# Branch b of a hybrid block in one kernel: its weights prepared by whole rows and stored by GpSimd, its products ordered by output pair, and w_out's banks taken in another order

## The chip, the cores and the metric

The kernel runs on one core of a Trainium2 chip. The metric is the device time of one execution in microseconds (us), lower is better. A core has five engines that run their own instruction streams: TensorE (PE, matrix products, with PEld for its weight loads), VectorE (DVE, elementwise work), ScalarE (ACT, activations and copies), GpSimd (POOL) and SyncE (SP, here only an issuer of DMAs). ScalarE and GpSimd issue DMAs too; a DMA is issued in the order of its engine's stream. TensorE writes into PSUM, of which there are eight banks of 128 x 512 float32; operands lie in SBUF, in tiles of 128 partitions.

## The reference

One layer of a hybrid block on x of 1024 x 1024 float32: a mixer and a SwiGLU network, each with a norm before and behind it. What the change touches is the mixer:

```python
def mixer(h, w_in, b_f, conv_w, w_branch, w_out):
    proj = jnp.einsum("bsd,dn->bsn", h, w_in)
    q, k, v, f_logit, g_b, g_c, hc, gate_conv, gate_attn = jnp.split(proj, _SPLITS, axis=-1)
    ya = g_b * causal_depthwise_conv(g_c * hc, conv_w)
    ...
    yb = forgetting_attention(q.reshape(shp), k.reshape(shp), v.reshape(shp), logf)
    yb = yb.reshape(bsz, s_len, ATTN_WIDTH)
    ya_d = jnp.einsum("bsc,cd->bsd", ya, w_branch[0])
    yb_d = jnp.einsum("bsc,cd->bsd", yb, w_branch[1])
    merged = jax.nn.sigmoid(gate_conv) * ya_d + jax.nn.sigmoid(gate_attn) * yb_d
    return jnp.einsum("bsd,de->bse", merged, w_out)
```

`yb` is 1024 x 512, `w_branch[1]` 512 x 1024, `w_out` 1024 x 1024.

## The kernel before, in words

**Arithmetic.** Each float32 product is made of three matmuls on rounded halves: an operand is split into a high half (a rounding copy by ScalarE) and a low half (a subtraction by VectorE), `split` (L132), and `mm3` (L137) multiplies high by high, high by low and low by high. The large products go by Strassen and Winograd: the operands are cut into 2 x 2 blocks, and seven products of sums of blocks (A11 B11, A12 B21, S1 T1, S2 T2, S3 T3, S4 B22, A22 T4) take the place of eight. A matmul has 128 x 128 weights and 128 x 512 data. All instructions of these helpers are put down to line 77 in the profile, so its rows are told apart by their tiles.

**Stages.** First the norm and v; then 18 jobs of the input projection (L1031: four of q and k, six of the convolution, eight of the gates, the last one run into the attention); attention with branch a's products as filler (L1341); branch b (L1502 to L1570); the w_out stage (L1722); then the feed-forward network.

**Order.** The instructions of an engine run in a fixed order. A planner lays it down at build time from its own costs, except where `strict` names the engine or a call is `pinned` (L119): those instructions keep the order of the program. In the jobs only a few are pinned; in the attention all engines are; in branch b from L1527 on only TensorE is. So VectorE's, ScalarE's and SyncE's orders in the jobs and in branch b are the planner's. An instruction that waits holds up all that stands behind it on its engine.

**Side work in the jobs.** While a job's 84 matmuls run, weights for later stages are prepared. `wo_load` (L965) loads four blocks of w_out, cuts sums and halves, and stores them to `wo_dram`; `wb_load` (L992) does the same for `w_branch[1]`: eight times four DMAs of a 128 x 128 block into a tile `br` (tag "p", two buffers), four sums of 128 x 128 on VectorE, a split of 128 x 896 into `bh` and `bl` (tag "cb", two buffers), and two stores to `wb_dram` issued by ScalarE, 512 bytes a piece. They are run in jobs 2 to 9. `cb_of` (L746) loads a row of forget sums, broadcast to 128 partitions, into buffers of the same tag "cb"; for the first head pair this is called at job 12 (L1068), ahead of the weight loads of that job, which `pairs.get()` (L679) issues one job ahead of use.

**Branch b.** The weights of the seven products (o = A11 to S4) come back from `wb_dram` by `load_wbr` (L1277): the high half into a ring of four buffers (`hi_t`), the low half into a ring of three (`lo_t`), for S1 into a tile of its own. `prod_b` (L1488) makes the product of o for one pair u of output blocks: 6 matmuls. The products run one after the other, each over u = 0 to 3: A11, S1, S2, S3, S4, A22, A12. Two sets of four PSUM banks, `pbanks` and `vbanks`, hold partial sums; `p_s`, `u_s`, `v_s` are copies of them in SBUF. After S3, S4, A22 and A12 VectorE adds the bank and merges: times the gate `sg` (loaded by SyncE into four buffers, `gate`, L1481), added to `um`. Each output block of `um` is done by one of these four products: S3 and S4 finish the columns n1, A22 and A12 the columns n2.

**The w_out stage** begins with `first(0)` (L1621): its bank comes from a new pool of four (`pk`, L1579) that lies on the first four of the eight banks of branch b's pool, and must wait until the last reader of that bank is done. Before, the eight banks were given in the order: three to branch a, four `pbanks`, four `vbanks`, the last three of them on banks 0, 1 and 2.

Of the kernel before, what the change touches and what calls it, by code (L numbers as in the profile page):

```python
# [10 lines left out]
F32 = mybir.dt.float32  # L11
# [6 lines left out]
P = 128  # L18
S = 1024
# [21 lines left out]


B11, B21, B22, T1, T2, T3, T4 = range(7)
A11, A12, A22, S1, S2, S3, S4 = range(7)


@with_exitstack
def block_kernel(
# [83 lines left out]
    def split(hi, lo, src):  # L132

        copy(hi, src)
        sub(lo, src, f32(hi))
# [23 lines left out]
    pre_dram = [dpool.tile([2, P, NC], F32, name=f"pre_dram{f}") for f in range(NPRE)]  # L159
    ri_dram = [dpool.tile([2, S], F32, name=f"ri_dram{j}") for j in range(4)]  # L160
    wo_dram = dpool.tile([7, 4, P, 2, NC], F32, name="wo_dram")
    wb_dram = dpool.tile([7, 2, P, 4, 2, P], F32, name="wb_dram")
    sg_dram = [dpool.tile([2, P, S], F32, name=f"sg_dram{d}") for d in range(8)]

    cw = cpool.tile([P, 4, 4], F32, name="cw")[:, :3, :]
# [372 lines left out]
    def kblk(t):  # L538
        return t.rearrange("p (a b) -> p a b", b=P)
# [7 lines left out]
    def hi_t():  # L547
        return wtile("hi", 4, F32R)
# [416 lines left out]
    def wo_load(n):  # L965
# [23 lines left out]

        return cut, store  # L990

    def wb_load(n):  # L992

        u, kk = divmod(n, 2)
        r = kblk(t0_.tile([P, S], F32, tag="p", name="br", bufs=2))
        h, l = (kblk(t0_.tile([P, S], F32R, tag="cb", name=x, bufs=2)) for x in ("bh", "bl"))
        blocks_ = ((kk, 2 * u + 1), (kk, 2 * u), (2 + kk, 2 * u), (2 + kk, 2 * u + 1))
        for slot, (row, col) in enumerate(blocks_):
            pinned(
                lambda: nc.sync.dma_start(  # L1000
                    r[:, slot],
                    w_branch[0, 1][row * P : (row + 1) * P, col * P : (col + 1) * P],
                ),
                "sync",
            )

        def cut():
            add(r[:, 4], r[:, 0], r[:, 3])
            sub(r[:, 6], r[:, 1], r[:, 0])
            sub(r[:, 5], r[:, 4], r[:, 1])  # L1010
            sub(r[:, 7], r[:, 2], r[:, 5])
            split(h[:, 1:], l[:, 1:], r[:, 1:])

        def store():
            for hl, t in enumerate((h, l)):
                nc.scalar.dma_start(
                    wb_dram[:, hl, :, u, kk, :].rearrange("o p m -> p o m"), f32(t[:, 1:])
                )

        return cut, store  # L1020
# [3 lines left out]
    def do(f, *args):  # L1024
        return lambda: f(*args)

    zts = {}
    h1b = [hB11, hB21, hB22]
    for hh, hl in (hT12, hT34):
        h1b += [(hh[:, b], hl[:, b]) for b in range(2)]  # L1030
    for ij, (kind, j, _, _) in enumerate(jobs):  # L1031
# [12 lines left out]
        if ij < 2:  # L1044
            if ij == 0:
                r1 = raw_t()
                nc.sync.dma_start(r1, kmaj(wcols(jobs[1][2])))
                t0_.tile([P, S], F32, tag="p", name="room", bufs=2)
                h1, l1 = (
                    kblk(t0_.tile([P, S], F32R, tag="cb", name=n, bufs=2)) for n in ("h1", "l1")  # L1050
                )
                split(h1, l1, r1)
                heads = [prep_first(None, t) for t in ((r0, h0, l0), (r1, h1, l1))]
                for _ in range(2):
                    bank(psm, "spare")
                strict[0] = ("tensor", "scalar")
                firsts = strassen_firsts([w for w, _ in heads], h1b, psm, pp)
                strict[0] = ()
            (w, r1), (c11, p1) = heads[ij], firsts[ij]
            w = {**w, **prep_rest(wcols(jobs[ij][3]), r1)}  # L1060
            if ij == 1:
                pairs.q.append(pairs.prep(*pairs.srcs.popleft()))
            _, c12, c21, c22 = strassen(w, h1b, psm, pp, p1, mid)
        elif ij < len(jobs) - 1:
            if ij == 12:
                k_load(0)
                q_load(0)
                cb_of(0, 0)  # L1068
                cb_of(0, 1)
            c11, c12, c21, c22 = strassen(pairs.get(), h1b, psm, pp, None, mid)  # L1070
        else:
            w = pairs.get()
            psm_close()
            strict[0] = engines
            pss, pss_close = pool("pss", space=PSUM)
            c11, c12, c21, c22 = last_pair(w)
# [41 lines left out]
            pinned(store, "scalar")  # L1118
        if ij < len(jobs) - 2:
            side[ij + 1].append(wo_load(ij))  # L1120
        if 1 <= ij < 9:
            side[ij + 1].append(wb_load(ij - 1))
    pp_close()
    w0_close()
    h_close()
# [149 lines left out]
        return t.rearrange("p (k a) b -> p k (a b)", k=2)  # L1275

    def load_wbr(o):  # L1277
        h = hi_t()
        l = kblk(z_tile("wbl", F32R)) if o == S1 else lo_t()
        wb[o] = h, l  # L1280
        for hl, t in enumerate((h, l)):
            nc.sync.dma_start(
                f32(t).rearrange("p (u k) m -> p u k m", u=4), wb_dram[o, hl]
            )

    low_k, up_k = slice(0, 2), slice(2, 4)
    yb11, yb12 = yb[:, low_k, n2], yb[:, low_k, n1]
# [41 lines left out]
        at[t].append(do(load_sg, d))  # L1329
    at[18] += [do(cb_of, 3, 0, True), do(cb_of, 3, 1, True)]  # L1330
    at[20].append(form_t1)
    for o, t in ((A11, 19), (S1, 20), (S2, 24), (S3, 25)):
        at[t].append(do(load_wbr, o))
    rows = {9: 0, 15: 1, 21: 2}
    for t, j in rows.items():
# [152 lines left out]
    def prod_b(ps, o, u, b, first):  # L1488
        (wh, wl), (bh, bl) = wb[o], tb[b]
        kw = {} if first else dict(skip_group_check=True)  # L1490
        for k in range(2):
            m = 2 * u + k
            mm3(
                ps, (wh[:, m, :], wl[:, m, :]), (bh[:, k, :], bl[:, k, :]),
                first and k == 0, k == 1, **kw,
            )

    def merge(d, ns, t, c, sg):
        mul(t, c, sg)
        add(um[:, d, ns], um[:, d, ns], t)  # L1500

    for m in branch_a(KT - 1, 0, psm, "mm"):  # L1502
        pass
    for n in range(2):
# [13 lines left out]
    for u in range(4):  # L1518
# [4 lines left out]
            sub(yb22, yb22, yb11)  # L1523
        if u == 1:
            split(*tb[T2], yb22)
    load_wbr(S4)
    strict[0] = ("tensor",)  # L1527
    divide(3, 1)
    yh1, yl1 = halves_of(1)
# [13 lines left out]
        load_wo(B11, u)  # L1543
    load_wbr(A22)
    for u in range(4):
        prod_b(pbanks[u], S2, u, T2, False)
        copy(u_s[u], pbanks[u])
    load_wbr(A12)
    for u in range(4):
        sg = gate(2 * u + 1, n1)  # L1550
        prod_b(pbanks[u], S3, u, T3, False)
        add(v_s[u], v_s[u], pbanks[u])
        merge(2 * u + 1, n1, v_s[u], v_s[u], sg)
    for u in range(4):
# [606 lines left out]
```

## Time and profile before

| | us |
|---|---|
| median of 3 runs | 1340.06 (1337.64 to 1340.38) |
| profiled execution | 1339.44 |
| its span, first to last instruction | 1337.7 |
| TensorE busy | 1308.7 (98%) |
| VectorE busy | 983.8 (74%) |
| ScalarE busy | 567.8 (42%) |
| GpSimd busy | 141.8 (11%) |

In a row of a timeline stand the start from the span's start, the duration, the engine, the operation, out<-in, and in brackets the idle time of the engine before it with what ended it; a q behind the engine's name (SPq, ACTq) is its queue of DMA issues. In a table by windows each engine has its busy time and count, then come the clock granted to TensorE (1.00 is full), the mean share of the DMA engines, and GB/s. A matmul's own duration (0.39 us) is longer than the step to the next one, since they are pipelined.

### The profile page before, as it was taken

The numbers are of one execution on the slowest core, as the hardware profiler recorded it, in microseconds if no ns is written. First come the engines' busy times: TensorE is split into PE (matmuls) and PEld (weight loads), VectorE is DVE, ScalarE is ACT, GpSimd is POOL, SyncE is SP. The second block draws the span as 40 slices with busy tenths as digits, with TensorE's granted clock in tenths as the row PEclk, the third lists the DMA queues.
The fourth block names the chain that finished last, engine by engine and source line by source line (L and its number), as shares of the span: only waits on it lengthen the run. The fifth ranks groups of instructions, "written<-read, shape, count | busy, mean of one in ns | idle before, by whom it ended". The sixth has DMA issues, their size and how long they took to land.

```text
span 1337.7 us, 18116 instructions
## 1 busy us (share of the span) xinstructions
PE 1308.7 (98%) x6686; PEld 1087.5 (81%) x6686; DVE 983.8 (74%) x1549; ACT 567.8 (42%) x902; POOL 141.8 (11%) x271
## 2 busy tenths in 40 slices
PE   9999999979999999997999999999999999999998
PEld 8988877768888888886888888888888888888886
DVE  6975889756555877578599689897677766677585
ACT  6642333324335766443577523232222323444452
POOL 0011000001102212001012112220011101000000
PEclk9999999989999999998999999999999999999999
DMA  6337667686555544598256645553233327876541
GB/s 219 114 116 195 195 184 208 168 226 170 163 152 183 192 135 138 180 340 321 93 190 220 189 150 173 182 180 96 101 116 105 108 98 264 315 272 194 158 165 63
DMA packets 223817, 235.14 MB, mean 176 GB/s; under 512 B 12512, under 2 KB 169248, under 8 KB 223728
## 3 DMA queue, kind: packets, MB, share of 16 engines
q1 hardware_dynamic: 163456, 157.13, 37.7%
q0 software_dynamic: 16496, 54.83, 11.2%
q10 hardware_dynamic: 43776, 22.02, 6.3%
q8 instruction: 52, 0.85, 0.3%
q14 instruction: 37, 0.30, 0.1%
HBM read 161.79 MB, written 72.16 MB: 175 GB/s over the span
## 4 chain that ended last, share of the span: by engine, by line
PE 77%; issue 13%; DMA 4%; DVE 4%; ACT 1%; POOL 1%; SPq 0%; DVEq 0%; POOLq 0%; ACTq 0%
PE b L77 42%; PE pd L77 16%; PE pba L77 3%; PE pv L77 3%; PE p L77 2%; PE po L77 2%; PE tps L77 2%; PE sp L77 2%; PE pbp L77 1%; DMA wb_dram<-bl 1%; PE ma L77 1%; PE q L77 1%; PE tp L77 1%; DMA lo<-qk_dram 1%; DMA raw<-in_w_in_dram 1%
## 5 line engine op out<-in xcount | busy, mean ns | idle before, releaser
L77 PE MATMUL b<-x,hi 128*128 128x512 f32 x1088 | 335.5, 389 | 0.0
L77 PEld LDWEIGHTS b<-x,hi 128*128 128x128 f32 x1088 | 204.1, 188 | 42.4
L77 PE MATMUL b<-x,lo 128*128 128x512 f32 x544 | 211.7, 389 | 0.0
L77 DVE TENSOR_TENSOR c<-c,b 128x512 f32<-128x512 f32 x193 | 131.0, 680 | 50.3 <-PE b L77 43.6
L77 DVE TENSOR_TENSOR lo<-raw,hi 128x1024 fp32r<-128x1024 f32 x90 | 108.2, 1202 | 71.5 <-PE b L77 61.2
L77 ACT ACTIVATE hi<-raw 128x1024 fp32r<-128x1024 f32 (+1 forms) x96 | 97.2, 1015 | 85.1 <-PE b L77 46.4
L77 PEld LDWEIGHTS b<-x,lo 128*128 128x128 f32 x544 | 102.1, 188 | 21.1
L77 ACT ACTIVATE hi<-sx 128x1024 fp32r<-128x1024 f32 (+1 forms) x42 | 43.7, 1040 | 137.0 <-PE b L77 122.7
L77 ACT ACTIVATE sgf<-c 128x512 f32<-128x512 f32 x31 | 19.6, 632 | 131.6 <-DVE c L77 112.5
L77 DVE TENSOR_TENSOR sx<-raw 128x512 f32<-128x512 f32 x78 | 53.5, 686 | 29.3 <-DMA raw<-in_w_in_dram 19.9
L77 DVE TENSOR_TENSOR lo<-sx,hi 128x1024 fp32r<-128x1024 f32 (+1 forms) x42 | 50.3, 1197 | 25.7 <-PE b L77 24.0
L77 PE MATMUL pd<-hi,lo 128*128 128x512 f32 x160 | 62.3, 389 | 0.0
L77 PE MATMUL pd<-hi 128*128 128x512 f32 x160 | 61.9, 390 | 0.0
L77 PE MATMUL b<-hT12h,lo 128*128 128x512 f32 x136 | 54.0, 397 | 6.5 <-DVE lo L77 6.5
L77 PE MATMUL pd<-ghi 128*128 128x512 f32 x148 | 57.6, 389 | 0.0
L77 PE MATMUL pd<-ghi,glo 128*128 128x512 f32 x148 | 57.6, 389 | 0.0
L77 PE MATMUL pd<-glo,ghi 128*128 128x512 f32 x148 | 57.6, 389 | 0.0
L77 PE MATMUL b<-hT34h,hi 128*128 128x512 f32 x136 | 53.4, 393 | 1.6 <-DVE c L77 1.6
L77 PE MATMUL b<-hT12h,hi 128*128 128x512 f32 x136 | 53.6, 394 | 0.0
L77 PE MATMUL b<-hT12l,hi 128*128 128x512 f32 x136 | 53.6, 394 | 0.0
L77 PE MATMUL b<-hT34l,hi 128*128 128x512 f32 x136 | 53.0, 389 | 0.0
L77 PE MATMUL b<-hT34h,lo 128*128 128x512 f32 x136 | 52.9, 389 | 0.0
(456 smaller groups left out, 3047.9 us busy)
## 6 DMA issues: line engine op xcount, KB each, us to landing
raw<-in_w_gate_up_dram SPq DMA_DIRECT2D x55, 512.0 KB, 3.9
raw<-in_w_in_dram SPq DMA_DIRECT2D x35, 512.0 KB, 5.4
x<-wo_dram SPq DMA_DIRECT2D x28, 512.0 KB, 7.2
a_dramS<-um POOLq DMA_DIRECT2D x44, 256.0 KB, 3.0
a_dramA<-um POOLq DMA_DIRECT2D x33, 256.0 KB, 2.8
sg<-sg_dram SPq DMA_DIRECT2D x32, 256.0 KB, 3.8
wo_dram<-h ACTq DMA_DIRECT2D x16, 448.0 KB, 4.6
wo_dram<-l ACTq DMA_DIRECT2D x16, 448.0 KB, 7.0
```

The source lines that it names most:

```text
L77: ins = getattr(self.engine, name)(*args, **kw)
```

## The change

Four things. (1) `wb_load` loads two whole rows of blocks (128 x 1024 each) at n = 0 and n = 4 and works on them in four steps each: split A12 and A22; split A11 and make the four sums in place; split S2 and S3; split S4 and S1. The names' numbers are changed so that the pairs lie side by side in `wb_dram`, now in pieces of 2 KB, and the stores are issued by GpSimd. The work lies in jobs 2 to 5 and 10 to 13. (2) The first `cb_of` loads move from job 12 to job 15, behind `pairs.get()`. (3) In branch b, S2, S4 and S3 run pair by pair, then A22 and A12 pair by pair; S4's weights are loaded during the attention in place of S3's, S3's behind A11's products, and A12's go into two buffers of the tag "raw" (three buffers, which B11's and T1's data held before). (4) Five unused banks are taken first, so that `pbanks` are banks 0 to 3 and `vbanks` banks 4 to 7.

```diff
-A11, A12, A22, S1, S2, S3, S4 = range(7)
+A11, A12, A22, S2, S3, S4, S1 = range(7)
...
-    wb_dram = dpool.tile([7, 2, P, 4, 2, P], F32, name="wb_dram")
+    wb_dram = dpool.tile([7, 2, P, 2, NC], F32, name="wb_dram")
...
     def wb_load(n):
-        u, kk = divmod(n, 2)
-        r = kblk(t0_.tile([P, S], F32, tag="p", name="br", bufs=2))
-        h, l = (kblk(t0_.tile([P, S], F32R, tag="cb", name=x, bufs=2)) for x in ("bh", "bl"))
-        blocks_ = ((kk, 2 * u + 1), (kk, 2 * u), (2 + kk, 2 * u), (2 + kk, 2 * u + 1))
-        for slot, (row, col) in enumerate(blocks_):
-            pinned(
-                lambda: nc.sync.dma_start(
-                    r[:, slot],
-                    w_branch[0, 1][row * P : (row + 1) * P, col * P : (col + 1) * P],
-                ),
-                "sync",
-            )
+        kk, c = divmod(n, 4)
+        if c == 0:
+            wrows[:] = [t0_.tile([P, S], F32, tag="p", name="br", bufs=2) for _ in range(2)]
+            for row, t in zip((kk, 2 + kk), wrows):
+                pinned(
+                    lambda: nc.sync.dma_start(t, w_branch[0, 1][row * P : (row + 1) * P, :]),
+                    "sync",
+                )
+        (r11, r21), (r12, r22) = (
+            [t.rearrange("p (u x m) -> x p u m", x=2, m=P)[x] for x in range(2)] for t in wrows
+        )
+        h, l = (t0_.tile([P, S], F32R, tag="cb", name=x, bufs=2) for x in ("bh", "bl"))
+        width = NC if c == 1 else S
+        first = (A12, A11, S2, S4)[c]
 
         def cut():
-            add(r[:, 4], r[:, 0], r[:, 3])
-            sub(r[:, 6], r[:, 1], r[:, 0])
-            sub(r[:, 5], r[:, 4], r[:, 1])
-            sub(r[:, 7], r[:, 2], r[:, 5])
-            split(h[:, 1:], l[:, 1:], r[:, 1:])
+            if c == 1:
+                hs, ls = (t[:, n1].rearrange("p (u m) -> p u m", m=P) for t in (h, l))
+                split(hs, ls, r11)
+                add(r22, r21, r22)
+                sub(r21, r11, r21)
+                sub(r11, r22, r11)
+                sub(r12, r12, r11)
+            else:
+                hs, ls = (t.rearrange("p (x u m) -> p x u m", x=2, m=P) for t in (h, l))
+                src = wrows[c != 2].rearrange("p (u x m) -> p x u m", x=2, m=P)
+                split(hs, ls, src)
 
         def store():
             for hl, t in enumerate((h, l)):
-                nc.scalar.dma_start(
-                    wb_dram[:, hl, :, u, kk, :].rearrange("o p m -> p o m"), f32(t[:, 1:])
+                nc.gpsimd.dma_start(
+                    wb_dram[first : first + width // NC, hl, :, kk, :].rearrange("o p c -> p o c"),
+                    f32(t[:, :width]).rearrange("p (o c) -> p o c", c=NC),
                 )
...
+    WB_AT = (2, 3, 4, 5, 10, 11, 12, 13)
...
             if ij == 12:
                 k_load(0)
                 q_load(0)
+            w = pairs.get()
+            if ij == 15:
                 cb_of(0, 0)
                 cb_of(0, 1)
-            c11, c12, c21, c22 = strassen(pairs.get(), h1b, psm, pp, None, mid)
+            c11, c12, c21, c22 = strassen(w, h1b, psm, pp, None, mid)
...
-        if 1 <= ij < 9:
-            side[ij + 1].append(wb_load(ij - 1))
+        if ij + 1 in WB_AT:
+            side[ij + 1].append(wb_load(WB_AT.index(ij + 1)))
...
     def load_wbr(o):
-        h = hi_t()
-        l = kblk(z_tile("wbl", F32R)) if o == S1 else lo_t()
+        if o == A12:
+            h, l = (wtile("raw", 3, F32R) for _ in range(2))
+        else:
+            h = hi_t()
+            l = kblk(z_tile("wbl", F32R)) if o == S1 else lo_t()
...
-    for o, t in ((A11, 19), (S1, 20), (S2, 24), (S3, 25)):
+    for o, t in ((A11, 19), (S1, 20), (S2, 24), (S4, 25)):
...
+    for _ in range(5):
+        bank(psm, "spare")
     for m in branch_a(KT - 1, 0, psm, "mm"):
...
-    load_wbr(S4)
+    load_wbr(S3)
+    load_wbr(A12)
...
     load_wbr(A22)
     for u in range(4):
+        sg2, sg1 = (gate(2 * u + x, n1) for x in range(2))
         prod_b(pbanks[u], S2, u, T2, False)
         copy(u_s[u], pbanks[u])
-    load_wbr(A12)
-    for u in range(4):
-        sg = gate(2 * u + 1, n1)
-        prod_b(pbanks[u], S3, u, T3, False)
-        add(v_s[u], v_s[u], pbanks[u])
-        merge(2 * u + 1, n1, v_s[u], v_s[u], sg)
-    for u in range(4):
-        sg = gate(2 * u, n1)
         prod_b(vbanks[u], S4, u, B22, False)
         add(u_s[u], u_s[u], vbanks[u])
         copy(vbanks[u], p_s[u])
-        merge(2 * u, n1, u_s[u], u_s[u], sg)
+        merge(2 * u, n1, u_s[u], u_s[u], sg2)
+        prod_b(pbanks[u], S3, u, T3, False)
+        add(v_s[u], v_s[u], pbanks[u])
+        merge(2 * u + 1, n1, v_s[u], v_s[u], sg1)
         load_wo(B21, u)
...
     for u in range(4):
-        sg = gate(2 * u + 1, n2)
+        sg1, sg2 = (gate(2 * u + 1 - x, n2) for x in range(2))
         prod_b(pbanks[u], A22, u, T4, False)
-        merge(2 * u + 1, n2, sg, pbanks[u], sg)
-    for u in range(4):
-        sg = gate(2 * u, n2)
+        merge(2 * u + 1, n2, sg1, pbanks[u], sg1)
         prod_b(vbanks[u], A12, u, B21, False)
-        merge(2 * u, n2, sg, vbanks[u], sg)
+        merge(2 * u, n2, sg2, vbanks[u], sg2)
```

More of the change, by code (lines that the diff above doesn't have):

```diff
@@ L990, in wo_load @@
         return cut, store
+    wrows = []
     def wb_load(n):
-        u, kk = divmod(n, 2)
-        r = kblk(t0_.tile([P, S], F32, tag="p", name="br", bufs=2))
-        h, l = (kblk(t0_.tile([P, S], F32R, tag="cb", name=x, bufs=2)) for x in ("bh", "bl"))
-        blocks_ = ((kk, 2 * u + 1), (kk, 2 * u), (2 + kk, 2 * u), (2 + kk, 2 * u + 1))
-        for slot, (row, col) in enumerate(blocks_):
-            pinned(
-                lambda: nc.sync.dma_start(
-                    r[:, slot],
-                    w_branch[0, 1][row * P : (row + 1) * P, col * P : (col + 1) * P],
-                ),
-                "sync",
-            )
@@ L1277, in load_wbr @@
     def load_wbr(o):
-        h = hi_t()
-        l = kblk(z_tile("wbl", F32R)) if o == S1 else lo_t()
+        if o == A12:
[3 more added lines that the diff above has]
+            l = kblk(z_tile("wbl", F32R)) if o == S1 else lo_t()
         wb[o] = h, l
         for hl, t in enumerate((h, l)):
-            nc.sync.dma_start(
-                f32(t).rearrange("p (u k) m -> p u k m", u=4), wb_dram[o, hl]
-            )
+            nc.sync.dma_start(flat(f32(t)).rearrange("p (k c) -> p k c", k=2), wb_dram[o, hl])
     low_k, up_k = slice(0, 2), slice(2, 4)
@@ L1491, in prod_b @@
         for k in range(2):
-            m = 2 * u + k
+            m = 4 * k + u
             mm3(
```

## The prediction

> **What bounds the kernel now.** I read the page first (busy shares), then the waits of TensorE, then the windows and timelines around its two long waits.
>
> ```profile
> PE 1308.7 (98%) x6686; PEld 1087.5 (81%) x6686; DVE 983.8 (74%) x1549; ACT 567.8 (42%) x902; POOL 141.8 (11%) x271
> ...
> PE p L77 <- DVE sg L77: 6.8, 1, 6.8
> PE b L77 <- DVE lo L77: 6.5, 1, 6.5
> PE b L77 <- ACT c L77: 3.0, 3, 1.3
> PE b L77 <- DVE c L77: 1.6, 2, 1.4
> ```
>
> TensorE is the bound: it is busy for 98% of the span, so only what makes it wait, or run slowly, can be won. Its waits are few: one of 6.8 us at the end of branch b, one of 6.5 us in the projections, five short ones of 4.6 us together. The diff touches the places of all of them. The windows add a second price:
>
> ```profile
> core 0: us, PE busy (x) PEld busy (x) DVE busy (x) ACT busy (x) POOL busy (x), PEclk, DMA share, GB/s
> 286.00:293.00 7.00, 0.54 (x3) 0.11 (x1) 4.00 (x6) 1.69 (x2) 0.54 (x1) 0.68 0.37 117
> 293.00:296.00 3.00, 2.92 (x7) 2.34 (x8) 2.27 (x5) 1.75 (x3) 0.54 (x1) 0.50 1.12 257
> 296.00:299.00 3.00, 3.00 (x9) 2.32 (x8) 1.62 (x3) 0.00 (x0) 0.00 (x0) 0.53 0.94 269
> 608.00:615.00 7.00, 0.25 (x2) 0.00 (x0) 5.92 (x9) 0.00 (x0) 1.05 (x2) 0.84 0.83 275
> 615.00:617.00 2.00, 1.93 (x5) 1.55 (x6) 2.00 (x5) 0.00 (x0) 0.00 (x0) 0.50 0.95 330
> 617.00:619.00 2.00, 2.00 (x6) 1.59 (x5) 2.00 (x4) 0.31 (x1) 0.00 (x0) 0.50 1.02 375
> 619.00:621.00 2.00, 2.00 (x9) 1.56 (x8) 2.00 (x4) 2.00 (x3) 0.00 (x0) 0.84 1.02 338
> ```
>
> After each long wait the granted clock (the column behind the engines) is about half for a while. Lost there: 3 x (1 - 0.50) + 3 x (1 - 0.53) = 2.9 us after the first wait, 2 x 0.50 + 2 x 0.50 + 2 x 0.16 = 2.3 us after the second. So the two waits cost 6.5 + 2.9 = 9.4 and 6.8 + 2.3 = 9.1 us.
>
> Beside these rows: TensorE: Matmul & The Clock Gate of the Trainium skill (Part 1, what's actually happening) has the clock halved after an idle window of about 3.4 us and restored after one busy window of that length. By that figure half speed would cost 1.7 us each time, an estimate from that page, and the sum below would come out 1.8 us smaller, at about 1320.4. The trace has durations for the same thing, and they are larger, so they stand.
>
> **Part 1: the wait in the projections.** What holds it is seen in the queue of SyncE, then ScalarE, then VectorE:
>
> ```profile
> 269.74 0.33 SPq L77 DMA_DIRECT2D q<-qk_dram  x1
> 278.15 1.64 SPq L77 DMA_DIRECT2D cb<-c_dram  x2
> 279.89 0.64 SPq L77 DMA_DIRECT2D raw<-in_w_in_dram  x1
> ...
> 266.63 1.05 ACTq L77 DMA_DIRECT2D wb_dram<-bh  x1
> 267.78 3.28 ACTq L77 DMA_DIRECT2D wb_dram<-bl  x1
> 271.61 1.06 ACT L77 ACTIVATE hi<-sx 128x1024 fp32r<-128x1024 f32 x1 [6.10 <-DMA wo_dram<-l]
> ...
> 289.00 0.69 DVE L77 TENSOR_TENSOR sx<-raw 128x512 f32<-128x512 f32 x1 [11.03 <-DMA raw<-in_w_in_dram]
> ...
> 291.81 1.22 DVE L77 TENSOR_TENSOR lo<-raw,hi 128x1024 fp32r<-128x1024 f32 x1
> ...
> 293.08 0.80 PE L77 MATMUL b<-hT12h,lo 128*128 128x512 f32 x1 [6.54 <-DVE lo L77]
> ```
>
> The two cb loads go into the buffers out of which bh and bl are stored (one tag, two buffers), and SyncE stands from 270.07 to 278.15 until the stores have been read out. The next weights (raw) queue behind them; VectorE, which keeps its order, sits 11.03 us at an operation on those weights, and TensorE's lo (291.81) stands behind that operation. The change moves the cb loads from job 12 to job 15, behind that job's weight loads. The raw load can then go right after 270.07, 9.8 us earlier. The chain behind it is shorter by more than the 6.5 us that TensorE waits, so the wait goes and its 2.9 us of slow clock too: 9.4 us. What is late next: TensorE's own pace, since VectorE had 11 idle us there. In job 15 the cb loads wait for nothing: by then the last branch-b store, of job 13, is a whole job old (a job is 84 matmuls; 24 take 5.44 us by the chain's rows below, so 19 us).
>
> **Part 2: stores off ScalarE's queue.** The last wb_dram issues above end at 271.06, and only then ScalarE makes hi<-sx, for which TensorE waits:
>
> ```profile
> L77 ACTq DMA_DIRECT2D wb_dram<-bh x8: 367/728/1054, 124.2 to 266.6; - x8
> L77 ACTq DMA_DIRECT2D wb_dram<-bl x8: 367/1506/3276, 126.6 to 267.8; - x8
> ...
> 248.00 0.63 ACT L77 ACTIVATE s4h<-s 128x512 fp32r<-128x512 f32 x1 [4.94 <-DMA wo_dram<-l]
> ...
> 249.17 0.50 PE L77 MATMUL b<-hB21h,hi 128*128 128x512 f32 x1 [1.29 <-ACT c L77]
> ...
> 265.53 0.77 POOL L77 DMA_DIRECT2D ya_dram<-c  x1 [10.51 <-DVE c L77]
> 268.19 0.54 POOL L77 DMA_DIRECT2D ya_dram<-c  x1 [1.89 <-DVE c L77]
> ...
> 160.00:270.00 110.00, 106.76 (x465) 86.48 (x464) 94.21 (x163) 34.00 (x40) 4.61 (x8) 1.00 0.70 187
> ```
>
> Sixteen issues at medians of 0.73 and 1.51 us are some 18 us of ScalarE's queue; they go to GpSimd, busy for 11% of the span, at about 0.54 us each. What they store is first loaded a whole attention stage later. The five short waits (4.6 us) lie in jobs where ScalarE stood at such issues; I take 4.4 as won (the one of 1.6 - 1.4 = 0.2 us is too short to place), with 0 and 4.6 as the ends. The w_out stores stay on ScalarE.
>
> The cutting costs VectorE much the same: eight times four small sums and a 128x896 split before; now, twice, three 128x1024 splits of 1.22 us (row 291.81), one of 512 and four 128x512 sums of 0.69 (row 289.00): 2 x 7.1 = 14.2 us in all. It has 26% idle, and the jobs with the convolution (6 to 9) get none of it. Its largest piece, 3.4 us in one job, is covered by the 11 us above; uncovered it would cost its own length twice. SyncE issues 4 row loads in place of 32 blocks; the two of jobs 1 and 9 put 1 MB ahead of a weight load, some 3 us at the rates of 257 to 375 GB/s in the windows. The weights are wanted a job ahead, so nothing by my sum; 3 us each if VectorE again stands in front of something urgent.
>
> **Part 3: branch b.**
>
> ```profile
> 570.17 5.44 PE pbp L77 x24
> 575.61 5.44 PE pbv L77 x24
> 581.05 6.82 PE pbp L77 x30
> ...
> 587.89 0.69 DVE L77 TENSOR_TENSOR temps<-temps,pbp 128x512 f32<-128x512 f32 x1 [7.85 <-PE pbp L77]
> ...
> 589.32 0.69 DVE L77 TENSOR_TENSOR temps<-temps,pbp 128x512 f32<-128x512 f32 x1
> 589.92 0.68 DVE L77 TENSOR_TENSOR um<-um,temps 128x512 f32<-128x512 f32 x1
> ...
> 614.32 0.69 DVE L77 TENSOR_TENSOR sg<-pbv,sg 128x512 f32<-128x512 f32 x1 [1.08 <-DMA sg<-sg_dram]
> ...
> 615.07 1.22 PE L77 MATMUL p<-x,s4h 128*128 128x512 f32 x2 [6.82 <-DVE sg L77]
> ```
>
> Seven products of 24 matmuls at 5.44 us run without a hole from 570.17 to 608.25. VectorE has nothing until 587.89, where the fourth product's first pair ends, and then 40 operations at one per 0.60 us (589.32 to 589.92), so it is 7 us behind at the end. The first bank of the w_out stage is one that VectorE empties at 614.32, in the last round.
>
> By the new order, a pair u takes 18 matmuls, 4.08 us, and gives VectorE six operations, 3.6 us; in the last two products 12 matmuls, 2.72 us, and four operations, 2.4 us. VectorE starts at 581.05 + 2.72 = 583.8 and keeps up. ScalarE's copy of S2's sum must end within S4's six matmuls, 1.36 us; ScalarE is nearly idle there, and if it is late, TensorE waits four times for the excess. With five spare banks ahead, w_out's four first banks are those of A22's products, the first of which is merged some 8 us before the end. Its operands need only the n1 merges, done three operations behind 597.4, near 599.5. So the 6.8 us and the 2.3 us of slow clock go: 9.1 us.
>
> It adds one wait. The low half of A22's weights takes a buffer of a ring of three; A12 no longer draws from that ring, and the order is A11, S2, S4, S3, A22, so A22's stands in S2's place. S2 now ends not with its block but with the last u:
>
> ```profile
> 586.52 0.33 SPq L77 DMA_DIRECT2D lo<-wb_dram  x1
> ...
> lo<-wb_dram SPq DMA_DIRECT2D x1, 512.0 KB, 4.2
> x<-wo_dram SPq DMA_DIRECT2D x24, 512.0 KB, 7.2
> ```
>
> Before, that load went at 586.52, as S2's block ended, and A22 came at 597.4. Now S2 ends at 581.05 + 3 x 4.08 + 1.36 = 594.65, and A22's first matmul with the low half is due at 597.37 + 0.45 = 597.8. With 4.2 us to landing it is there at 598.9: 1.1 us of TensorE's time; with the 7.2 us of loads of the same size in this stretch, 4.1 us; nothing if the stage is already late otherwise. I take 1.5, nearest to the row of the same load, with something for SyncE being at another issue. Behind that waiting load stand the gate loads on SyncE. No slow clock: in the window 160 to 270 above, with most of the short waits (1.29 us at 249.17), the granted clock is 1.00.
>
> **The sum.** The profiled execution took 1339.44 us (span 1337.7, and 1.7 around it); the median of the runs shown is 1340.06, 0.6 above it. 9.4 + 4.4 + 9.1 - 1.5 = 21.4 us less: 1318.0, and with the 0.6 a median of 1318.6 us. Behind branch b all moves forward with TensorE; I take w_out's weights as loaded in time, since no wait of TensorE is for them now.
>
> **The rivals.**
> - The short waits stay, since the w_out stores alone hold ScalarE as long. For it: those issues too last up to 1.5 us; against it: the short waits all lie where both kinds of stores share the queue. 1318.6 + 4.4 = 1323.0.
> - Branch b's tail stays: one late gate load makes VectorE, in its fixed order, late at every bank, or A22's low half comes as late as 4.1 us and the clock falls. For it: there are four gate buffers, and VectorE already waits 1.08 us for a gate load in the last round (614.32). The first form gives 1339.44 - 9.4 - 4.4 + 0.6 = 1326.2.
> - The wait in the projections comes back behind the row loads (1 MB ahead of a weight load in job 9), with its slow clock: 1318.6 + 9.4 = 1328.0. Against it: the weights are loaded a job ahead.
> - No change: both long waits come back at new places, since the order of VectorE's work is laid down anew: 21.4 - 9.4 - 9.1 = 2.9 us are left, about the 0.2%.
> - Slower: GpSimd's queue hands bh and bl back too late. Its place is jobs 10 to 13, where four gate stores a job stand in the same queue. The cut of the next job starts some 19 us after the last one, so this decides only if a store lands more than about 13 us late; then ScalarE and VectorE stand at the buffers in three hand-overs, each like the wait at 286: 3 x 9.4 = 28.2, 1318.0 + 28.2 + 0.6 = 1346.8. Against it: GpSimd's issues above, 0.54 us and at worst 0.77. Beside that: DMA: Bandwidth & Descriptors of the Trainium skill (SWDGE vs HWDGE) says that VectorE in its two-port mode locks GpSimd out of the descriptors it must write. By that rule stores would be late in the jobs with VectorE's short single-source operations; the 0.77 is the most that this trace could show of it, and it isn't near the point.
>
> **How the numbers follow.** Forecast 0.57, short waits stay 0.13, tail stays 0.12, projections' wait returns 0.09, no change 0.03, slower 0.06. Faster by over 0.2% (2.7 us, what a measurement of this kernel can tell): 0.57 + 0.13 + 0.12 + 0.09 = 0.91; same 0.03; slower 0.06. Low end: without A22's wait 1317.1, less about 3 for the spread of the runs: 1314. High end: the third rival, 1328.0, and one more for that spread: 1329.
>
> **What would show it.** Right: no wait of TensorE over 2 us between 60 and 300 us; SyncE not standing at cb; wb_dram stored from GpSimd's queue; no wait on "sg" in front of w_out, which starts near 596 (608.25 less the 13.8 us won ahead, and A22's 1.5 us on it), at full clock; a short wait on "lo" loaded from wb_dram in front of A22. Wrong: granted clock near 0.5 anywhere in those stretches, VectorE late at the gates, or ScalarE still at DMA issues in front of the short waits.

## The result, and the profile after

The changed kernel took 1318.79 us (median of 4 runs, 1317.89 to 1321.7), the kernel before 1339.24 us beside it: ratio 0.9852, 95% interval 0.9832 to 0.9872. The forecast was 1318.6. The profiled execution took 1317.89 us, its span 1316.1, which is 21.6 us under the span of before; the forecast sum was 21.4. By the medians the gain is 20.5 us. The number is right; the experiments show that three of the steps behind it are not.

Busy shares of the page, then the waits of TensorE in the changed kernel (us in total, times, longest):

```profile
PE 1302.1 (99%) x6686; PEld 1084.9 (82%) x6686; DVE 981.7 (75%) x1525; ACT 567.6 (43%) x902; POOL 153.8 (12%) x287
```

```profile
PE p L77 <- DVE sg L77: 1.6, 1, 1.6
...
PE pbp L77 <- DMA lo<-wb_dram: 1.2, 1, 1.2
...
PE b L77 <- ACT c L77: 0.4, 1, 0.4
```

Both long waits and nearly all of the short ones are gone; TensorE has 1.6 us for a gate and 1.2 us for A22's low half instead. Where the time was won is seen by setting the same matmul of the two timelines side by side. This is the last one ahead of the long wait of before, in the kernel before and in the changed one:

```profile
286.15 0.39 PE L77 MATMUL b<-hT12l,hi 128*128 128x512 f32 x1
```

```profile
279.25 0.39 PE L77 MATMUL b<-hT12l,hi 128*128 128x512 f32 x1
```

So 6.9 us are won ahead of it. At the first product of branch b, in the chain of the changed kernel, it is 570.17 - 554.52 = 15.65 us:

```profile
554.52 5.44 PE pbp L77 x24
559.96 5.44 PE pbv L77 x24
```

and at the end 21.6. The projections gave 15.65 (forecast 13.8), branch b and the step into w_out 5.95 (forecast 7.6). The end of branch b, in the timeline of the changed kernel:

```profile
579.03 0.32 SPq L77 DMA_DIRECT2D lo<-wb_dram  x1
...
590.66 2.72 SPq L77 DMA_DIRECT2D sg<-sg_dram  x3
...
593.95 0.62 PE L77 MATMUL p<-x,s4h 128*128 128x512 f32 x2
...
597.04 0.63 ACT L77 ACTIVATE sg<-sg 128x512 f32<-128x512 f32 x1 [8.80 <-issue]
...
597.71 0.69 DVE L77 TENSOR_TENSOR sg<-pbp,sg 128x512 f32<-128x512 f32 x1 [1.73 <-ACT sg L77]
...
598.45 0.74 PE L77 MATMUL p<-x,hi 128*128 128x512 f32 x2 [1.62 <-DVE sg L77]
```

w_out's first product starts at 593.95 with no wait. Its second one waits 1.62 us for the product of the last A22 pair with its gate. That gate is the second of the three loads in the row at 590.66: it is issued at 592.46, when one of the four gate buffers comes free, and lands at 596.97, 4.5 us later; its sigmoid follows at 597.04, and VectorE's product at 597.71.

### The profile page after: what moved, and what is told of

Read it like the earlier page. It is cut to its first block, busy times and chain, and to the rows that moved or that the text cites. A ratio compares the mean times of both kernels' runs of the same rounds, so it can differ in the third digit from the quotient of the medians.

```text
span 1316.1 us, 18049 instructions
## 1 busy us (share of the span) xinstructions
PE 1302.1 (99%) x6686; PEld 1084.9 (82%) x6686; DVE 981.7 (75%) x1525; ACT 567.6 (43%) x902; POOL 153.8 (12%) x287
## 4 chain that ended last, share of the span: by engine, by line
PE 72%; issue 18%; DVE 3%; DMA 3%; POOL 2%; ACT 1%; SPq 0%; DVEq 0%; POOLq 0%; ACTq 0%
PE b L77 37%; PE pd L77 16%; PE pba L77 3%; PE pv L77 3%; PE tps L77 2%; PE po L77 2%; PE p L77 2%; PE sp L77 2%; PE pbp L77 1%; PE ma L77 1%; PE q L77 1%; PE tp L77 1%; POOL wb_dram L77 1%; PE pbv L77 1%; DMA wb_dram<-bl 1%
```

## The experiments

Twelve kernels ran, each timed beside the kernel before (1338.38 us for e1 to e4, 1337.69 for e6 to e9, 1337.84 for e10 to e13).

| run | what differs | us | ratio to before (95%) |
|---|---|---|---|
| e1_cb_only | before, cb call at job 15 | 1338.91 | 1.0001 (0.9993 to 1.001) |
| e7_cb_pinned | before, cb loads held at job 15 | 1331.04 | 0.9952 (0.9938 to 0.9965) |
| e8_jobs_only | before, weights in jobs 2 to 5, 10 to 13 | 1330.87 | 0.9954 (0.9941 to 0.9966) |
| e2_gpsimd_only | before, stores on GpSimd | 1346.93 | 1.0065 (1.0051 to 1.0079) |
| e3_order_only | before, branch b as changed | 1333.27 | 0.9965 (0.9952 to 0.9977) |
| e4_rows_scalar | changed, stores on ScalarE | 1320.88 | 0.9871 (0.9857 to 0.9884) |
| e12_rows_small | e4 with 512-byte pieces | 1322.98 | 0.989 (0.9877 to 0.9903) |
| e9_rows_old_jobs | changed, jobs 2 to 9 | 1320.9 | 0.9874 (0.9861 to 0.9888) |
| e6_a22_z | changed, A22's low half in its own tile | 1321.08 | 0.9878 (0.9864 to 0.9891) |
| e10_banks | the same program as the changed kernel | 1318.92 | 0.9868 (0.9851 to 0.9885) |
| e11_banks_z | the same program as e6 | 1321.77 | 0.9883 (0.9867 to 0.99) |
| e13_order_banks | the same program as e3 | 1334.49 | 0.9976 (0.9966 to 0.9986) |

### The cb loads: e1 and e7

e1 makes the change's part (2) alone; e7 also holds the loads at that place.

```diff
+            w = pairs.get()
+            if ij == 15:
                 cb_of(0, 0)
                 cb_of(0, 1)
-            c11, c12, c21, c22 = strassen(pairs.get(), h1b, psm, pp, None, mid)
+            c11, c12, c21, c22 = strassen(w, h1b, psm, pp, None, mid)
```

```diff
+                for e in range(2):
+                    pinned(lambda: cb_of(0, e), "sync")
```

> The kernel before with one edit: the first two loads of forget-sum rows move from job 12 to job 15, behind that job's weight loads. Theory (SyncE stands at these loads until the branch-b stores are read out, and the weight load behind them is late): the wait of TensorE in front of lo near 286 us goes, with its slow clock, and nothing else: 9.4 us less, near 1330. Rival (the stores on ScalarE's queue are the cause, the loads are only in the same place): the wait stays or shrinks by less than half, 0 to 4 us less.

Nothing moved in e1. SyncE's timeline shows why: the planner put the loads where they were, ahead of the same raw load. The two kernels are the same program, instruction for instruction, so that e1 is a repeat of the kernel before.

```profile
271.31 0.33 SPq L77 DMA_DIRECT2D q<-qk_dram  x1
279.85 1.63 SPq L77 DMA_DIRECT2D cb<-c_dram  x2
281.58 1.06 SPq L77 DMA_DIRECT2D raw<-in_w_in_dram  x1
```

> The kernel before, with the two cb loads at job 15 and pinned there in SyncE's order (moving the call alone left them where they were). Theory (SyncE standing at the cb loads holds the raw load, VectorE and TensorE): the wait of TensorE for lo near 286 us goes with its slow clock, 9.4 us less, about 1329, ratio 0.993; the five short waits stay. Rival (the long wait comes from VectorE's order or from ScalarE at the store issues): the wait stays at 4 us or more, and the gain is under 4 us.

With the loads held back, SyncE goes on to the raw load, and the wait for lo is gone from TensorE's list. SyncE's timeline, then the waits:

```profile
270.69 0.33 SPq L77 DMA_DIRECT2D q<-qk_dram  x1
274.87 0.38 SPq L77 DMA_DIRECT2D raw<-in_w_in_dram  x1
```

```profile
PE p L77 <- DVE sg L77: 7.3, 1, 7.3
PE b L77 <- ACT c L77: 3.8, 3, 1.5
PE b L77 <- DVE c L77: 1.9, 2, 1.4
```

The gain is 6.65 us by the medians (4.7 to 8.3 by the interval), and 8.8 by the spans of the two profiled executions (1337.7 and 1328.9). So the chain SyncE, raw, VectorE, lo is the cause of that wait; the call at job 15 isn't what removes it in the change.

### The jobs and the stores' issuer: e8 and e2

e8 gives the kernel before the changed places of the side work and the cb call, e2 gives it GpSimd's stores. Blocks, sums and pieces stay.

```diff
+    WB_AT = (2, 3, 4, 5, 10, 11, 12, 13)
...
-        if 1 <= ij < 9:
-            side[ij + 1].append(wb_load(ij - 1))
+        if ij + 1 in WB_AT:
+            side[ij + 1].append(wb_load(WB_AT.index(ij + 1)))
```

```diff
-                nc.scalar.dma_start(
+                nc.gpsimd.dma_start(
                     wb_dram[:, hl, :, u, kk, :].rearrange("o p m -> p o m"), f32(t[:, 1:])
```

> The kernel before with the side work of branch b's weights in jobs 2 to 5 and 10 to 13 (blocks and ScalarE's 512-byte stores as before), and the cb call at job 15. The planner then puts the cb loads late, since their buffers are in use until job 13. Theory (the placement alone takes the long wait away, the size of the pieces makes the short ones): the 286 us wait goes (9.4 us), short waits remain, now in jobs 10 to 13 too, so about 1329 to 1331, ratio 0.993 to 0.994. Rival (the jobs are what makes the short waits, since the convolution's jobs have the most store issues on ScalarE): short waits go as well, about 1323, ratio 0.988. Second rival (the long wait is a matter of the stores' pieces): it comes back in jobs 10 to 13, and nothing is gained.

The long wait is gone here too: with stores up to job 13 the buffers of cb are taken until then, and the planner puts the loads behind them. The short waits stay (of before: 3.0 and 1.6 us in five), in jobs 11 to 13 as well:

```profile
PE b L77 <- ACT c L77: 5.4, 5, 1.3
...
PE b L77 <- DVE lo L77: 1.1, 1, 1.1
```

What ScalarE does at one of them, and at its longest issue, with SyncE's loads ahead, from the timelines of e8:

```profile
185.07 0.99 ACTq L77 DMA_DIRECT2D wb_dram<-bh  x1
186.19 4.05 ACTq L77 DMA_DIRECT2D wb_dram<-bl  x1
...
276.94 2.44 SPq L77 DMA_DIRECT2D r<-in_w_out_dram  x4
...
279.49 0.96 ACT L77 ACTIVATE bh<-br 128x896 fp32r<-128x896 f32 x1 [0.95 <-DVE br L77]
...
282.83 0.39 ACTq L77 DMA_DIRECT2D wb_dram<-bh  x1
283.88 0.63 ACT L77 ACTIVATE s4h<-s 128x512 fp32r<-128x512 f32 x1 [2.91 <-DMA r<-in_w_out_dram]
...
285.04 0.50 PE L77 MATMUL b<-hB21h,hi 128*128 128x512 f32 x1 [1.30 <-ACT c L77]
```

bh is made at 280.45, but its store is issued only at 282.83, and the profile puts ScalarE's idle time down to the loads r. The program says why: the DMAs of SyncE and ScalarE take one of eight completion counts in turn, and each is issued only when the one eight places earlier has landed; for this store that is the second of the four r loads, issued at 277.32 and landed at 282.75. With block loads a job has fourteen such DMAs, so eight places back is a load just issued. At 184 to 190 us it has another form: four stores are issued within 2.2 us (183.99 to 186.19), and the issues come out longer and longer, up to 4.05 us.

> The kernel before with one edit: the branch-b stores, still in blocks and pieces of 512 bytes, are issued by GpSimd. Theory (ScalarE standing at the issues makes the short waits): the short waits between 160 and 275 us go, 4.4 to 6 us less; and as the last stores are issued some 3 us sooner, SyncE is released sooner, the long wait near 286 us shrinks from 6.5 to 2 or 3 us and loses its slow clock: 11 us less in all, near 1328. Rival (pieces of 512 bytes make the stores land late from any queue): the long wait stays with its slow clock, only 4.4 to 6 us less, near 1334.

e2 is slower than before by 8.6 us (0.65%), and neither the theory nor the rival foresaw why. GpSimd takes 0.95 us for each issue, and it holds each of these stores, of 896 pieces, apart from its other DMAs: in all 23 places where one stands next to another DMA of GpSimd between 120 and 300 us, the later of the two goes 0.3 us or more after the earlier has landed. So bl goes 8.4 us after bh, and a store of the convolution, ya_dram<-ot, ready at 193.43, goes at 198.17. VectorE needs that store's buffer back and sits idle for 4.95 us (1.74 before); from there it works without a pause until TensorE has waited for its c. Rows of GpSimd, VectorE and TensorE in e2:

```profile
185.83 0.95 POOL L77 DMA_DIRECT2D wb_dram<-bh  x1 [9.92 <-ACT bh L77]
194.26 0.94 POOL L77 DMA_DIRECT2D wb_dram<-bl  x1 [7.49 <-DVE ot L77]
198.17 0.59 POOL L77 DMA_DIRECT2D ya_dram<-ot  x1 [2.97 <-issue]
...
200.59 0.49 DVE L77 TENSOR_SCALAR ot<-zt,cw 128x512 f32<-128x512 f32 x1 [4.95 <-DMA ya_dram<-ot]
...
214.74 0.79 PE L77 MATMUL b<-hT34h,hi 128*128 128x512 f32 x1 [2.67 <-DVE c L77]
```

The same comes again at 264.49, and TensorE waits 2.85 us at 281.04; after both waits the clock is halved. By the same matmul in both timelines e2 is 0.2 us behind the kernel before at 205 us, 5.8 at 220 and 10.4 at 286, and its span is 10.9 longer. The chain of the cb loads comes on top, but adds less than 1 us of that: SyncE stands at both cb loads until GpSimd's late stores have landed (the last one at 291.12), and TensorE waits 7.7 us for lo. SyncE's timeline:

```profile
291.26 0.32 SPq L77 DMA_DIRECT2D cb<-c_dram  x1
291.68 0.38 SPq L77 DMA_DIRECT2D raw<-in_w_in_dram  x1
```

In the changed kernel the stores have 128 or 256 pieces and GpSimd doesn't hold them apart (bl goes at 182.13, bh of 179.62 lands at 187.44), and the work of jobs 6 to 9 has none of them.

### Whole rows: e4, e12 and e9

e4 puts the changed kernel's stores back on ScalarE; e12 also writes them in pieces of 512 bytes (and reads them back in pieces of 1 KB), with the order of instructions the same on every engine; e9 puts the changed kernel's side work back into jobs 2 to 9.

```diff
-                nc.gpsimd.dma_start(
+                nc.scalar.dma_start(
```

```diff
-    wb_dram = dpool.tile([7, 2, P, 2, NC], F32, name="wb_dram")
+    wb_dram = dpool.tile([2, 7, 4, P, 2, P], F32, name="wb_dram")
...
-                    wb_dram[first : first + width // NC, hl, :, kk, :].rearrange("o p c -> p o c"),
-                    f32(t[:, :width]).rearrange("p (o c) -> p o c", c=NC),
+                    wb_dram[hl, first : first + width // NC, :, :, kk, :].rearrange("o u p m -> p (o u) m"),
+                    f32(t[:, :width]).rearrange("p (q m) -> p q m", m=P),
```

```diff
-    WB_AT = (2, 3, 4, 5, 10, 11, 12, 13)
+    WB_AT = (2, 3, 4, 5, 6, 7, 8, 9)
```

> The changed kernel with one edit: the branch-b stores, by rows and in pieces of 2 KB, are issued by ScalarE again. Theory as predicted (ScalarE standing at DMA issues makes the short waits): they come back, 4.4 to 6 us more than the changed kernel, near 1324. Rival (it is the number of pieces, a quarter of what it was, that made the issues long): issues of about 0.4 us, no short waits, 0 to 1 us more, near 1319.

> The kernel with row stores on ScalarE (e4), but wb_dram laid out so that each store is written in pieces of 512 bytes in place of 2 KB; the order of instructions is the same on every engine, the loads back come in pieces of 1 KB. Theory (small pieces make ScalarE's issues long, and that makes the short waits): issues of bh and bl reach 1 to 4 us, short waits of TensorE for ScalarE's and VectorE's copies come back in jobs 2 to 5 and 10 to 13, 4 to 7 us more than e4, ratio 0.990 to 0.992. Rival (the cut by whole rows, not the pieces, took the short waits away): at most 1 us more than e4, ratio 0.987 to 0.988.

> The changed kernel with the side work of branch b's weights back in jobs 2 to 9; whole rows, 2 KB pieces and GpSimd's stores are kept. The planner then puts the cb loads early in SyncE's order again, as in the kernel before. Theory (the cb loads waiting for stores of long duration make the long wait, and 2 KB pieces land sooner): SyncE stands shorter, no long wait or a short one, the short waits stay away: 0 to 4 us over the changed kernel, ratio 0.985 to 0.988. Rival (the placement of the jobs is what counts, through the convolution's jobs): the long wait is back with its slow clock, 9 us or more over the changed kernel, ratio 0.992.

The short waits stay away in all three: TensorE waits for c 0.6 us in e4 and in e12, and 1.5 us in three waits of at most 0.6 in e9; the long wait stays away too. By the interval e4 and e9 can't be told from the changed kernel and its repeat. So neither the issuer nor the jobs are needed for what was won. With ScalarE as issuer the pieces aren't either: the stores' issues (ns, shortest, median, longest) in e4, then in e12, are nearly the same. (Small pieces by whole rows from GpSimd weren't tried; e2 speaks against them.)

```profile
L77 ACTq DMA_DIRECT2D wb_dram<-bh x8: 569/582/757, 121.0 to 333.3; - x8
L77 ACTq DMA_DIRECT2D wb_dram<-bl x8: 338/366/436, 123.4 to 336.3; - x8
```

```profile
L77 ACTq DMA_DIRECT2D wb_dram<-bh x8: 575/580/882, 121.0 to 333.4; - x8
L77 ACTq DMA_DIRECT2D wb_dram<-bl x8: 366/366/367, 123.6 to 336.3; - x8
```

My theory for e12 fell: it is some 2 us slower than e4 by the medians (the intervals overlap), but not by the short waits: it waits 2.2 us for lo near 356 us, after SyncE stood at cb until 340.96, and 3.0 us for the gate in w_out (1.8 in e4). What e4, e9 and e12 have in common, and e2 and e8 lack, is the load and cut by whole rows. What it changes on ScalarE is seen in e4 around the start of job 6 (178.7):

```profile
178.48 1.05 ACT L77 ACTIVATE bh<-br 128x1024 fp32r<-128x1024 f32 x1
...
183.21 0.37 ACTq L77 DMA_DIRECT2D wb_dram<-bl  x1
183.68 1.06 ACT L77 ACTIVATE hi<-raw 128x1024 fp32r<-128x1024 f32 x1 [4.15 <-DMA wo_dram<-h]
```

ScalarE stands here too: bl's store waits until wo_dram<-h of the same job has landed (183.13). But bh no longer waits for the block loads and sums of its own job, so the stores come earlier: the last one is issued by 298.00, 5.1 us into job 12, in e8 by 304.48, 8.7 us into it. That this lead is what spares TensorE the short waits is a reading of the traces; no run changes it alone.

### Branch b: e3 and e13, e6 and e11, e10

e3 is the kernel before with parts (3) and (4) alone. e6 is the changed kernel with one line more:

```diff
-            l = kblk(z_tile("wbl", F32R)) if o == S1 else lo_t()
+            l = kblk(z_tile("wbl", F32R)) if o in (S1, A22) else lo_t()
```

e10, e11 and e13 are the changed kernel, e6 and e3 with this:

```diff
+    pbanks = [pbanks[u] for u in (3, 1, 0, 2)]
...
+    vbanks = [vbanks[u] for u in (1, 0, 2, 3)]
```

> The kernel before with branch b's part of the change alone (pair order, loads of S4, S3 and A12, five spare banks); weights made and stored as before, forget-sum rows loaded at job 12 as before. Theory (the parts add up): 9.1 us of the tail and its slow clock go, A22's low half costs 1.2 us and the wait at the gate in front of the second w_out product 1.6 us: 6.1 to 6.5 us less, near 1333. Rival (part of the gain in branch b comes from what was won ahead of it, as loads reach it with more lead): under 4 us less.

> The kernel before with the branch-b part alone (e3) and the banks dealt as in e10. Theory (the 4.75 us gap that e3 kept at w_out's second product is the bank of the last A22 pair): the gap goes and its slow clock too, so the part gives the 9.1 us of the prediction less A22's wait, about 8.5, ratio 0.9935. Rival (late gate loads hold VectorE at every bank): the gap moves to a later product, ratio 0.996 as for e3.

> The changed kernel with one edit: A22's low half goes into a tile of its own kind in place of the ring of three, so that its load need not wait for S2's last product. Theory (that wait of TensorE, 1.2 us, is an effect of the ring, and the gate loads queue behind the waiting load): the wait goes and with it some of the 1.6 us wait at w_out's second product, so 1.2 to 2.8 us less than the changed kernel, ratio to the kernel before about 0.983 to 0.984. Rival (the gates' order alone sets the end of branch b): the A22 wait goes, but the wait at w_out's second product grows by as much, ratio 0.985 as for the changed kernel.

> As the run before, and A22's low half in a tile of its own. Theory: neither the wait in front of A22 nor that in w_out is left, branch b gives what the prediction's part 3 said, about 2.8 us less than the changed kernel, ratio about 0.983. Rival (the planner's order of the jobs shifts with any edit of the tiles and puts a wait of 1 to 2 us elsewhere, as when the tile was tried alone): one of the two gains is given back in the jobs, ratio 0.984 to 0.986.

> The changed kernel with the four pbanks and the four vbanks dealt to other u, so that the banks that w_out takes first (0, 3, 4, 2 by the program's memory map) belong to the pairs that end first; the unused banks are left as they are and change nothing in that map. Theory (w_out's second product waits for the bank of the last A22 pair, whose gate comes last): the 1.6 us wait goes, the 1.2 us wait for A22's low half stays; about 1.6 us less than the changed kernel, ratio about 0.984. Rival (the late gate holds VectorE, which is late at a later bank too): the wait moves to a later product of w_out, ratio 0.985 or above.

The dealing of the banks reached nothing, and its theory stays untried. A bank isn't given when a tile is named but when it is first written, so the three kernels are, instruction for instruction and bank for bank, the programs of the changed kernel, of e6 and of e3, and serve as their repeats. The same holds for the five unused banks of part (4): without them the program is the same, so part (4) and the order of the banks that is told ahead of the prediction aren't what the program does. In all of them, and in the kernel before, `pbanks` are banks 1, 2, 5, 3 in the order of u, `vbanks` 4, 0, 7, 6, and w_out takes 0, 3, 4, 2 first. Bank 0 is A12's second pair, bank 3 A22's last: that is the one whose gate comes late.

e3 won 5.1 us, its repeat 3.4: the new order takes away the 6.8 us, but the gate of the last A22 pair gives much of it back, 4.4 us and a slow clock in e3, 2.4 us in e13. The load of that gate took 6.5 us to land in e3 (605.86 to 612.36), 4.5 in the changed kernel. TensorE's waits in e3:

```profile
PE b L77 <- DVE lo L77: 5.2, 1, 5.2
PE p L77 <- DVE sg L77: 4.4, 1, 4.4
```

In e6 the wait in front of A22 is gone, and it is no faster than the changed kernel. The wait for the gate is 2.5 us (2.9 in e11), but the changed program has 1.6 in one execution and 2.9 in e10's, so that the gain is given back there, as the rival had it, isn't shown. What is seen is a loss elsewhere: a wait of 1.2 us for c in e6, of 2.5 us for lo in e11, both in the jobs, which the edit doesn't touch, and in both a halved clock behind the wait for the gate (below), which the changed kernel's profiled execution didn't have. No run was faster than the changed kernel.

## Why the prediction was right or wrong

- **The bound.** Right: TensorE goes from 98% to 99% busy, and what was won is waits and slow clock.
- **Part 1, 9.4 us.** The size and the chain were right: the matmuls behind that wait stand 16.4 us earlier than before, 9.5 more than the 6.9 ahead of it, and e7 shows the chain by cutting it. The failed step is "The change moves the cb loads from job 12 to job 15": e1 makes that edit alone and nothing moves. In the change two other parts each suffice: the later jobs (e8) and, with GpSimd's stores of larger pieces, the whole rows (e9, where the cb loads stay early but the last store is issued at 259.9 us and SyncE is past cb by 268.8). "In job 15 the cb loads wait for nothing" failed as well. They stand directly behind the raw load of 333.98, and wait for the two stores that GpSimd has just issued, one each (bh's lands at 339.88, bl's at 343.33); rows of GpSimd and SyncE in the changed kernel:

```profile
333.98 1.28 SPq L77 DMA_DIRECT2D raw<-in_w_in_dram  x1
...
334.68 0.71 POOL L77 DMA_DIRECT2D wb_dram<-bl  x1 [1.26 <-DVE bl L77]
...
340.16 3.65 SPq L77 DMA_DIRECT2D cb<-c_dram  x2
343.93 0.38 SPq L77 DMA_DIRECT2D raw<-in_w_in_dram  x1
```

  SyncE stands from 335.26 to 340.16, the old wait in small. It costs some 0.6 us near 358, and 2.5 in e11.
- **Part 2, 4.4 us.** Mis-sized and put down to the wrong cause: 6.9 us were won, and "stores off ScalarE's queue" isn't why (e4 wins as much with them on it). The four largest of the short waits were 1.20, 1.29, 1.68 and 1.75 us from start to start of matmuls, 5.0 us beyond the usual 0.23 each; the rest lay in delays too short for the list. ScalarE did stand at its store issues, as the quoted rows showed, but a releaser that is a DMA stood beside them, and I read all of it as the length of issues. That holds at 271.61, behind an issue of 3.28 us; at 248.00 it doesn't: the issue before it took 0.37 us, and ScalarE had stood from 244.30 until a block load eight places back had landed, at 247.52. What goes with the whole rows is the block loads (four DMAs a job), the bunch of four stores, and bh's wait for loads and sums of its own job. Which of them was worth most, the runs don't separate. VectorE kept pace, as forecast (981.7 us busy).
- **GpSimd's issues.** "About 0.54 us each" was somewhat low: 0.54 to 0.74 in the changed kernel, by tile:

```profile
L77 POOL DMA_DIRECT2D wb_dram<-bh x8: 540/716/735, 120.6 to 332.1; - x8
L77 POOL DMA_DIRECT2D wb_dram<-bl x8: 540/715/736, 121.9 to 334.7; - x8
```

  The rival "GpSimd's queue hands bh and bl back too late" did not come with the change, and e2 shows a queue of GpSimd that does harm in another way: with stores of 896 pieces the kernel is slower by 8.6 us, for the most part since the convolution's stores stand behind them, and only in a small part through the cb loads that wait for bh and bl. DMA: Bandwidth & Descriptors of the Trainium skill (Issuing engines are not separate DMA queues) says that a DMA moved to another engine saves only the time to issue it, usually small. e4 beside the changed kernel agrees (1320.88 and 1318.79 us, overlapping intervals). e2 beside the kernel before doesn't: there the move cost 8.6 us, and the measurement decides.
- **Part 3, 9.1 us.** Mis-sized: 5.95 won on the way into w_out, with A22's wait in it; without that 1.2 us it is some 7.2. The 6.8 us wait and its slow clock went. The failed step is "With five spare banks ahead, w_out's four first banks are those of A22's products": the spares change nothing, and the second bank that w_out takes is that of the last A22 pair. So the second rival's late gate load came in part, 1.6 us instead of a whole tail. w_out began at 593.95, not near 596, since 2 us more had been won ahead of it.
- **A22's low half, 1.5 us.** Right: 1.2 us, the load issued at 579.03 when S2's last product ended, and none with a tile of its own.
- **The sum.** 21.4 forecast, 21.6 by the spans: 2.5 us too little for the short waits, nearly made up by 1.6 us at the gate and 0.6 at job 15 that weren't in it. That these errors cancelled is luck. The 21.6 is of one execution each; repeats of the same program waited 1.6 and 2.9 us at that gate.

## What to carry to other kernels

Where a planner orders the instructions, moving a call in the text is no prediction of where its DMA goes: ask what its buffer waits for. An engine that stands "at a DMA issue" may be waiting for another DMA altogether; read the releaser, and count the DMAs of the job before blaming their length or their engine. Before a store moves to GpSimd, count its pieces, and see what else stands in GpSimd's queue. A sum that comes out right proves none of its terms: only single edits showed that one part of this change does nothing by itself (e1) and another does harm by itself (e2).

## What the runs showed of the hardware

**The clock after waits of 2 to 3 us.** The changed kernel's waits of 1.2 and 1.6 us cost no clock, and neither did 2.4 us in e13. e10 and e11 both waited 2.9 us at the same place of w_out; the windows behind it (in the column behind the engines the granted clock), in e10, then in e11:

```profile
599.00:601.00 2.00, 1.65 (x7) 1.39 (x8) 2.00 (x4) 0.00 (x0) 0.00 (x0) 1.00 1.05 405
```

```profile
601.00:603.00 2.00, 1.73 (x4) 1.44 (x5) 2.00 (x5) 0.00 (x0) 0.00 (x0) 0.50 1.06 410
603.00:605.00 2.00, 2.00 (x6) 1.52 (x6) 2.00 (x5) 0.68 (x1) 0.00 (x0) 0.50 1.05 407
605.00:607.00 2.00, 2.00 (x7) 1.52 (x6) 2.00 (x3) 2.00 (x4) 0.00 (x0) 0.50 1.08 391
```

After a wait of the same length the clock stayed full in one and halved in the other, which then lost about 3 x 2 x 0.50 = 3.0 us. A wait of 1.8 us at this place was enough in e4, and one of 2.5 us in e6. The windows of e4:

```profile
598.00:600.00 2.00, 0.94 (x3) 0.79 (x4) 1.68 (x3) 0.29 (x1) 0.00 (x0) 0.89 1.04 381
600.00:602.00 2.00, 2.00 (x6) 1.52 (x6) 2.00 (x5) 0.00 (x0) 0.00 (x0) 0.50 1.05 406
602.00:604.00 2.00, 2.00 (x9) 1.59 (x8) 2.00 (x5) 1.89 (x2) 0.00 (x0) 0.76 1.06 410
```

That is 2 x 0.11 + 2 x 0.50 + 2 x 0.24 = 1.7 us lost; e6 lost 1.7 us as well, and so did e3 behind its 4.4 us (2 x 0.40 + 2 x 0.46). TensorE: Matmul & The Clock Gate of the Trainium skill (Part 1, what's actually happening) has the clock fall after an idle window of some 3.4 us that runs freely. That a wait may or may not cost the clock fits it; that 1.8 us can be enough is shorter than its figure, and the measurement decides. An estimate from its figure, half speed for one such window, is 1.7 us lost, as in e3, e4 and e6; e11 lost nearly twice that.

**Issue time.** One store of 448 KB from ScalarE takes 0.37 us alone and up to 4.05 us as the fourth of four within 2.2 us (e8), for a reason that no run here takes apart; spread over 4.6 us (178.60 to 183.21 in e4) none of four took more than 0.58 us. The size of the pieces, 512 bytes or 2 KB, doesn't show in it (e4, e12). From GpSimd a store took 0.95 us with 896 pieces of 512 bytes (e2), 0.54 to 0.74 us with 128 or 256 pieces of 2 KB. The stores of 896 pieces never overlapped another DMA of GpSimd's (e2), those of 256 did (the changed kernel); where between the two this begins, and why, no run shows.
